# A gate/up product in seven block products (Strassen) instead of eight, with the trunk in DRAM during a feed-forward part

## The chip, the cores and the metric

The kernel runs on one core of one Trainium2 chip. The metric is device time in microseconds. Matrix products run on TensorE, elementwise work on VectorE and ScalarE, a little on GpSimd, and every DMA is issued by SyncE, in order, on one queue.

## The reference

Two layers of a diffusion trunk over 640 tokens: 512 of the sample and 128 of the prompt, width 1024, all in float32. Each layer has a feed-forward part (FFN), a token mix (two kinds of attention and a Fourier branch) and a second FFN; each of the three is followed by a LayerNorm over the sum with the trunk. Nine vectors per layer (the adaLN vectors: shift, scale and gate) come from a product of the conditioning vector with `w_mod`. An FFN with 2816 hidden columns is

```python
g, u = jnp.split(h @ w_gu, 2, axis=-1)
return (jax.nn.silu(g) * u) @ w_down
```

so that four FFNs run in all, and they hold most of the arithmetic.

## The kernel before

Activations lie transposed: 8 row blocks of 128 channels by 640 tokens, and the tokens in two halves of 320. A float32 product is made of rounded parts: `Unit` loads a weight block of up to 128 x 1024 and splits it into `hi`, cast by ScalarE (L149), and `lo`, the rest, subtracted by VectorE (L154); activations are split in the same way (`vsplit`, L109 and L110; `hh` and `hl` are the two parts of the input, `midh` and `midl` those of the hidden columns). `mm3` (L112) then issues three matmuls for each block of 128 x 128 weights and 320 tokens: hi by hi (L113), hi by the activations' lo (L114) and lo by hi (L115).

`ffn_steps` (L586) cuts the 2816 hidden columns into 22 tiles of 128. A tile's body multiplies 8 row blocks by the gate weights and 8 by the up weights, for two halves: 8 x 2 x 2 x 3 = 96 matmuls. `finish` (L593) applies SiLU on ScalarE and the product with `u` on VectorE (L599), and splits the result. After the first 11 tiles their part of the down product is formed, column by column (8 columns `m`, 11 x 2 x 3 matmuls each), and `plain_residual` (L711) adds it into the trunk, which stays in SBUF. After the other 11 tiles comes the second down part, with the LayerNorm: the last two columns are formed for half 0, then for half 1, so that half 0's LayerNorm can run beside half 1's matmuls (`LayerNorm.skewed`, L454); the last LayerNorm of all ends in the output (`finale`).

The conditioning work is spread through this. A `mod` of `mod_steps` (L254) is one 512 KB slice of `w_mod`, which VectorE multiplies and adds in two instructions of 1024 (L268 for the first slice of a vector, L270 for the others); after eight slices TensorE adds up and transposes (L274, L286), and VectorE writes the vector (L291). `with_mods` (L1723) places the slices evenly over the steps of an FFN.

The program is written as a list of steps, each with the weight units that it needs. `prep_to` (L162) loads and splits units ahead, at most `LOOK` = 4 units beyond the step, in rings of three raw and four hi/lo buffers. A scheduler then orders the instructions of each engine; the engines run theirs in order and wait on semaphores. Before a first FFN `startup` puts `w_mod` blocks into six slots; the token mix uses the rings' and the trunk's space for its own tiles.

Of the kernel before, what the change touches and what calls it, by code (L numbers as in the profile page):

```python
# [20 lines left out]
KT = 8  # L21
DEPTH = 2
NS = 512
# [5 lines left out]
PARTS = (11, 11)  # L29
MIDW = 11 * T  # L30
T_BUFS = 7
# [4 lines left out]
LOOK = 4  # L36
# [5 lines left out]
RAW_BUFS = 3  # L42
# [14 lines left out]
def trunk_kernel(ctx: ExitStack, tc: tile.TileContext, a, y_prompt, y_sample, new_a_k, new_a_v, new_b_k, new_b_v):  # L57
# [58 lines left out]

    class Unit:
# [3 lines left out]

        def prep(self):
            self.load()
            self.convert()

        def load(self):
            w = self.k * self.n
            if self.extra:
                raw = big.tile([128, 3 * T], F32, tag="xr", name="xr")[:, :w]
            else:  # L130
                raw = ring.tile([128, 1024], F32, tag="raw", name="raw")[:, :w]
# [9 lines left out]
        def high(self):  # L141
# [4 lines left out]
            else:  # L146
                hi = ring.tile([128, 1024], F32R, tag="hi", name="hi", bufs=HI_BUFS)[:, :w]
# [5 lines left out]
        def low(self):  # L153
            nc.vector.tensor_sub(self.l, self.raw, self.h)  # L154

# [6 lines left out]
    def prep_to(n):  # L162
        while ptr[0] < min(n, len(flat)):
            flat[ptr[0]].prep()
            ptr[0] += 1

# [3 lines left out]
    def step(units, fn):  # L170
        steps.append((units, fn, False))
# [23 lines left out]
    rope = const.tile([128, 2, NS], F32, name="rope")  # L195
# [58 lines left out]
    def mod_steps(l, j):  # L254
        out = []
        for k in range(KT):
# [3 lines left out]
            def fn(u=u, k=k):  # L260
# [10 lines left out]
                if k == KT - 1:  # L271
# [21 lines left out]
            out.append(([u], fn, False))  # L293
# [292 lines left out]
    def ffn_steps(l, which, gate_fn, pre=None):  # L586
        wgu = a[f"w_ffn{which}_gu"][l]
        wdn = a[f"w_ffn{which}_down"][l]
        gu = lambda t: (wunit(wgu, 0, KT, t * 128, 128), wunit(wgu, 0, KT, FFN + t * 128, 128))
        loc = {}  # L590
        ln = LayerNorm(l, 0 if which == 1 else 2, gate_fn)

        def finish(i, pg, pu):  # L593
            mh, ml = loc["mid"]
# [3 lines left out]
            for src, v in pu.pieces():  # L598
                nc.vector.tensor_mul(v(s), v(s), src)  # L599
            vsplit(mh[:, i, :], ml[:, i, :], s)  # L600
            return s
# [5 lines left out]

        t = 0
        for pi, n in enumerate(PARTS):
            for i in range(n):  # L610
                if t == 0:
# [16 lines left out]
                    steps.append(([u0[0], u0[1], u1[0]], head, bool(pre)))  # L628

                    def second(u1=u1):  # L630
# [3 lines left out]
                        finish(1, loc.pop("g1"), pu)  # L634

                    step([u1[1]], second)
                elif t > 1:
                    u = gu(t)

                    def body(u=u, i=i, last=(t == FT - 1)):  # L640
# [7 lines left out]
                        s = finish(i, pg, pu)  # L648
                        if last:
                            preload_rsqrt(s[:, 0:1])  # L650
                        if state["rescale"]:
                            state["rescale"].pop(0)()

                    step(list(u), body)
                t += 1
            k0 = t - n
            ka = n // 2
            final = pi == len(PARTS) - 1
            du = lambda m: [wunit(wdn, k0, ka, m * 128, 128), wunit(wdn, k0 + ka, n - ka, m * 128, 128)]

            def down_mm(us, out, hf, n, ka):
                mh, ml = loc["mid"]
                for k in range(n):
                    u, kk = (us[0], k) if k < ka else (us[1], k - ka)
                    mm3(out, u.h[:, kk, :], u.l[:, kk, :], mh[:, k, half(hf)], ml[:, k, half(hf)], k == 0, k == n - 1)

            nskew = (3 if ln.last else 2) if final else 0
            for m in range(KT - nskew):
                us = du(m)

                def body(us=us, m=m, n=n, ka=ka, final=final):
# [5 lines left out]
                    for hf in range(2):  # L677
                        down_mm(us, p.h[hf], hf, n, ka)
                    for hf in range(2):
                        if final:  # L680
                            ln.residual(m, hf, p.h[hf])
                        else:
                            plain_residual(m, hf, p.h[hf], gate_fn())

                step(us, body)
            if final:
                us = [wunit(wdn, k0 + k, min(4, n - k), (KT - 2) * 128, 256) for k in range(0, n, 4)]
                at = {(m, k): (us[k // 4], k % 4, 128 * (m - KT + 2)) for m in (KT - 2, KT - 1) for k in range(n)}
                if ln.last:
                    us = du(KT - 3) + us  # L690
                    us[0].extra = True
# [1136 lines left out]
```

## Time and profile before

| | us |
|---|---|
| three runs | 2567.93, 2566.44, 2567.11 (median 2567.11) |
| profiled execution, first to last instruction (its span) | 2563.8 |
| median less that span | 3.3 |
| TensorE busy | 2529.4 (99%) |
| VectorE busy | 1476.9 (58%) |
| ScalarE busy | 931.5 (36%) |
| mean granted clock of TensorE | 0.997 |

The profiled execution gives no time of its own beside its span; the span and the 3.3 us around it make up the median. Matmul records overlap, so the busy time of TensorE says when it has work and not how fast that work goes.

### The profile page before, as it was taken

Reading aid. Unit: us, or ns where it says so; the run is one execution under the profiler, and the core shown is the slowest. Engines: PE = TensorE matmul, PEld = TensorE weight load, DVE = VectorE, ACT = ScalarE, POOL = GpSimd, SP = SyncE. Lnnn points to the kernel's source line nnn. Section 1 sums busy time; section 2 is a strip of 40 time slices with the busy share of each in tenths; the row PEclk is TensorE's granted clock in tenths of the full one; section 3 lists DMA queues with packets and bytes.
Section 4 is the critical chain, followed back from the end, with each engine's and each line's share of the span. In section 5 each row is a group of like instructions: output and inputs, shape, how many; then the busy total and the mean of one; then the engine's idle time right before and its main releaser. Section 6 shows DMA issues by size and latency. Waiting matters only on the chain.

```text
span 2563.8 us, 41715 instructions
## 1 busy us (share of the span) xinstructions
PE 2529.4 (99%) x17407; PEld 2453.6 (96%) x17407; DVE 1476.9 (58%) x2522; ACT 931.5 (36%) x1714; POOL 40.3 (2%) x42
## 2 busy tenths in 40 slices
PE   8999999999999999999999999999999999999998
PEld 6999999999979999999999999999998899999998
DVE  5555644767967634433684465568678684232335
ACT  4221222366775421222262212225567662212221
POOL 0000000001100000000000000000110000000000
PEclk9999999999999999999999999999999999999999
DMA  9444543333122423433333354433411324122221
GB/s 265 144 122 134 156 124 106 116 121 86 35 84 88 141 74 101 123 91 94 111 107 116 106 157 136 132 114 107 125 50 49 113 75 132 56 85 83 71 83 56
DMA packets 371033, 273.64 MB, mean 107 GB/s; under 512 B 11162, under 2 KB 347804, under 8 KB 370332
## 3 DMA queue, kind: packets, MB, share of 16 engines
q1 hardware_dynamic: 370844, 270.98, 36.4%
q8 instruction: 136, 2.23, 0.4%
q14 instruction: 53, 0.43, 0.1%
HBM read 254.95 MB, written 9.18 MB: 103 GB/s over the span
## 4 chain that ended last, share of the span: by engine, by line
PE 89%; DVE 5%; ACT 2%; DMA 2%; SPq 1%; issue 1%; DVEq 0%; ACTq 0%
PE g L113 8%; PE g L114 8%; PE u L115 8%; PE g L115 8%; PE u L113 8%; PE u L114 8%; PE d L113 7%; PE d L114 7%; PE d L115 7%; PE b_o L1315 1%; PE a_o L1174 1%; PE o L113 1%; PE o L114 1%; PE o L115 1%; PE ps_v L937 1%; PE ps_v L938 1%
## 5 line engine op out<-in xcount | busy, mean ns | idle before, releaser
L149 ACT CAST hi<-raw 128x1024 fp32r<-128x1024 f32 (+4 forms) x355 | 336.6, 951 | 1249.2 <-PE u L114 414.6
L154 DVE TENSOR_TENSOR lo<-raw,hi 128x1024 fp32r<-128x1024 f32 (+4 forms) x355 | 390.0, 1100 | 371.1 <-ACT hi L149 369.8
L115 PE MATMUL u<-hh,lo 128*128 128x320 f32 x1408 | 435.2, 309 | 0.4 <-DVE lo L154 0.4
L114 PE MATMUL u<-hl,hi 128*128 128x320 f32 x1408 | 435.5, 309 | 0.0
L113 PE MATMUL u<-hh,hi 128*128 128x320 f32 x1408 | 435.2, 309 | 0.0
L113 PE MATMUL g<-hh,hi 128*128 128x320 f32 x1344 | 417.0, 310 | 0.0
L113 PE MATMUL d<-midh,hi 128*128 128x320 f32 x1342 | 416.1, 310 | 0.0
L115 PE MATMUL g<-hh,lo 128*128 128x320 f32 x1344 | 415.8, 309 | 0.0
L114 PE MATMUL g<-hl,hi 128*128 128x320 f32 x1344 | 415.2, 309 | 0.0
L114 PE MATMUL d<-midl,hi 128*128 128x320 f32 x1342 | 415.0, 309 | 0.0
L115 PE MATMUL d<-midh,lo 128*128 128x320 f32 x1342 | 414.8, 309 | 0.0
L270 DVE SCALAR_TENSOR_TENSOR acc<-raw,csil,acc 128x1024 f32<-128x1024 f32 x224 | 279.0, 1281 | 159.8 <-DMA raw<-in_w_mod_dram 159.7
L115 PEld LDWEIGHTS u<-hh,lo 128*128 128x128 f32 x1408 | 264.3, 188 | 0.8 <-DVE lo L154 0.6
L114 PEld LDWEIGHTS u<-hl,hi 128*128 128x128 f32 x1408 | 264.3, 188 | 0.2
L113 PEld LDWEIGHTS u<-hh,hi 128*128 128x128 f32 x1408 | 264.3, 188 | 0.0
L113 PEld LDWEIGHTS g<-hh,hi 128*128 128x128 f32 x1344 | 252.3, 188 | 8.0 <-issue 7.1
L113 PEld LDWEIGHTS d<-midh,hi 128*128 128x128 f32 x1342 | 251.9, 188 | 6.1 <-ACT hi L149 3.4
L115 PEld LDWEIGHTS g<-hh,lo 128*128 128x128 f32 x1344 | 252.3, 188 | 0.2
L114 PEld LDWEIGHTS g<-hl,hi 128*128 128x128 f32 x1344 | 252.3, 188 | 0.0
L114 PEld LDWEIGHTS d<-midl,hi 128*128 128x128 f32 x1342 | 251.9, 188 | 0.2
L115 PEld LDWEIGHTS d<-midh,lo 128*128 128x128 f32 x1342 | 251.9, 188 | 0.0
L599 DVE TENSOR_TENSOR silu<-silu,u 128x320 f32<-128x320 f32 x176 | 84.9, 486 | 255.6 <-PE u L115 254.1
(530 smaller groups left out, 3705.8 us busy)
## 6 DMA issues: line engine op xcount, KB each, us to landing
raw<-in_w_ffn_gu_dram SPq DMA_DIRECT2D x172, 512.0 KB
raw<-in_w_mod_dram SPq DMA_DIRECT2D x128, 512.0 KB
raw<-in_w_ffn_down_dram SPq DMA_DIRECT2D x60, 384.0 KB
raw<-in_w_ffn_down_dram SPq DMA_DIRECT2D x55, 320.0 KB
raw<-in_w_in_dram SPq DMA_DIRECT2D x24, 512.0 KB
raw<-in_w_out_dram SPq DMA_DIRECT2D x16, 512.0 KB
vtile<-vtile SPq DMA_DIRECT2D x40, 160.0 KB
st_midh<-in_w_mod_dram SPq DMA_DIRECT2D x10, 512.0 KB
```

Source lines behind the costliest of these rows:

```text
L113: nc.tensor.matmul(out, wh, xh, start=first, stop=False)
L114: nc.tensor.matmul(out, wh, xl, start=False, stop=False)
L115: nc.tensor.matmul(out, wl, xh, start=False, stop=last)
L149: nc.scalar.copy(hi, self.raw.rearrange("p k n -> p (k n)"))
L154: nc.vector.tensor_sub(self.l, self.raw, self.h)
L270: nc.vector.scalar_tensor_tensor(acc[:, s, :], w, cs, acc[:, s, :], op0=ALU.mult, op1=ALU.add)
L599: nc.vector.tensor_mul(v(s), v(s), src)
L937: nc.tensor.matmul(ps, hh[:, k, c], wh, start=(k == 0), stop=False)
L938: nc.tensor.matmul(ps, hl[:, k, c], wh, start=False, stop=False)
L1174: nc.tensor.matmul(x["po"][64 * r : 64 * r + 64, :128], M["va"][:, kt, 64 * g : 64 * g + 64], ph[:, c0 : c0 + 128], start=(kt == 0), stop= ...
L1315: nc.tensor.matmul(x["po"][:, 128 * q : 128 * q + 128], ph[:, c0 : c0 + 128], M["vb"][:, kt, 128 * h : 128 * h + 128], start=(kt == 0 and ...
```

## The change

Of an FFN's 22 tiles the first 10 (first FFN) or 5 (second FFN) stay as they were; the other 12 or 17 go through `seven`, 58 tiles in all. There the 8 row blocks are two groups of four (inputs' rows 1 and 2), and the two halves of tokens, and gate and up columns, make 2 x 2 blocks. Strassen's scheme (in Winograd's form) forms the four results from seven products of block sums, each of 4 row blocks x 3 matmuls = 12. `Pair` loads a gate and an up block into two raw buffers, splits the gate block and the second half of the up block, and then overwrites the raw buffers with sums of the blocks (`Sums`, split in their turn). `block_sums` makes the matching sums of activations: `t12` lies in the trunk's buffer, `t4` in a buffer called `xr`, and `t3` replaces the second half of the first four row blocks of `hh` and `hl` (`block_third`). Some products add into the PSUM tile of an earlier one, once VectorE or ScalarE has read the earlier value.

Since the trunk's buffer is taken, the trunk lies in DRAM during an FFN: eight tiles of 320 KB are stored (`park`), one is fetched, added to and stored again for each column of a down part that is not the last, and all return ahead of the last (`unpark`). The down product has three parts, of 8, 7 and 7 tiles. The `w_mod` slices are placed by rates: three to a plain tile, 1.25 and 1.75 to a column of the first FFN's down parts, one in the second FFN's, none in the tiles of seven products. Weights are prepared ahead as far as counts of held raw and hi/lo buffers allow (`advance`), with four raw buffers in place of three. The rope table is fetched into a ring buffer in each token mix instead of once, startup uses five slots, and some tiles of attention lie elsewhere.

```diff
-PARTS = (11, 11)
-MIDW = 11 * T
-T_BUFS = 7
+PARTS = (8, 7, 7)
+MIDW = max(PARTS) * T
+PLAIN = {1: 10, 2: 5}
+MOD_RATE = {1: (3.0, 1.25, 1.75), 2: (3.0, 1.0, 1.0)}
+T_BUFS = 9
...
-RAW_BUFS = 3
+RAW_BUFS = 4
...
+    class Pair(Unit):
+        def __init__(self, gate_src, up_src):
+            super().__init__(None, KT, 128)
+            self.pair = gate_src, up_src
+            self.raws = 2
+
+        def fetch(self):
+            self.g, self.u = (ring.tile([128, 1024], F32, tag="raw", name="raw") for _ in range(2))
+            for t, src in ((self.g, self.pair[0]), (self.u, self.pair[1])):
+                nc.sync.dma_start(out=t.rearrange("p (k n) -> p k n", k=KT), in_=src)
+
+        def convert(self):
+            held["raw"] += 1
+            self.raw = self.g.rearrange("p (k n) -> p k n", k=KT)
+            self.high()
+            u2 = ring.tile([128, 512], F32R, tag="hi2", name="hi2", bufs=2)
+            l2 = ring.tile([128, 512], F32R, tag="lo2", name="lo2", bufs=2)
+            g1, g2, u1, up = self.g[:, :512], self.g[:, 512:], self.u[:, :512], self.u[:, 512:]
+            nc.scalar.copy(u2, up)
+            self.low()
+            nc.vector.tensor_sub(l2, up, u2)
+            self.h2, self.l2 = (x.rearrange("p (k n) -> p k n", k=4) for x in (u2, l2))
+            nc.vector.tensor_add(up, up, u1)
+            nc.vector.tensor_add(u1, u1, g1)
+            nc.vector.tensor_add(g1, g1, up)
+            nc.vector.tensor_add(g2, g2, g1)
...
+        def convert(self):
+            self.raw = getattr(self.pair, self.which).rearrange("p (k n) -> p k n", k=KT)
+            self.high()
+            self.low()
...
+    def room(u):
+        return u.early and (u.loaded or held["raw"] + u.raws <= RAW_BUFS)
+
+    def advance():
+        while ptr[0] < len(flat):
+            u = flat[ptr[0]]
+            if not room(u) or u.extra or held["hi"] + u.his > HI_BUFS:
+                break
+            prep_to(ptr[0] + 1)
+        for u in flat[ptr[0] :]:
+            if not room(u):
+                break
+            u.load()
...
+        def park(n):
+            for _ in range(n):
+                state["rescale"].pop(0)()
+                k = KT - 1 - len(state["rescale"])
+                nc.sync.dma_start(out=parked[k], in_=state["trunk"][:, k, :])
+
+        def fetch(m):
+            xt[m] = t640(f"xt{m}")
+            nc.sync.dma_start(out=xt[m], in_=parked[m])
+
+        def unpark():
+            new_trunk()
+            for k in range(KT):
+                nc.sync.dma_start(out=state["trunk"][:, k, :], in_=parked[k])
...
+        def block_sums(k):
+            if k == 0:
+                t12 = big.tile([128, KT * T], F32R, tag="trunk", name="t12")
+                t4 = big.tile([128, 4 * T], F32R, tag="xr", name="t4")
+                loc["t12"] = [x.rearrange("p (k t) -> p k t", k=4) for x in (t12[:, : 4 * T], t12[:, 4 * T :])]
+                loc["t4"] = [x.rearrange("p (k t) -> p k t", k=4) for x in (t4[:, : 4 * HW], t4[:, 4 * HW :])]
+                loc["t3"] = []
+            if k % 2 == 0:
+                loc["t3"].append(t640(f"t3_{k}"))
+            t3 = loc["t3"][k // 2][:, half(k % 2)]
+            hh, hl = state["hh"], state["hl"]
+            f, g = t640(f"tf{k}"), t640(f"tg{k}")
+            nc.vector.tensor_add(f, hh[:, k, :], hl[:, k, :])
+            nc.vector.tensor_add(g, hh[:, k + 4, :], hl[:, k + 4, :])
+            f0, f1, g0, g1 = f[:, :HW], f[:, HW:], g[:, :HW], g[:, HW:]
+            nc.vector.tensor_sub(t3, g1, f1)
+            nc.vector.tensor_sub(f0, f0, f1)
+            nc.vector.tensor_add(f1, f0, g1)
+            nc.vector.tensor_sub(g0, f1, g0)
+            vsplit(loc["t12"][0][:, k, :], loc["t12"][1][:, k, :], f)
+            vsplit(loc["t4"][0][:, k, :], loc["t4"][1][:, k, :], g0)
+
+        def block_third():
+            for i, t3 in enumerate(loc["t3"]):
+                dh, dl = (state[key][:, 2 * i : 2 * i + 2, HW:] for key in ("hh", "hl"))
+                vsplit(dh, dl, two(t3))
+
+        def seven(i, us, last):
+            pair, sg, su = us
...
+            ab = mmp.tile([128, 2, 512], F32, tag="mm", name="ab")
+            cd = mmp.tile([128, 2, 512], F32, tag="mm", name="cd")
+            pa, pb, pc, pd = ab[:, 0, :HW], ab[:, 1, :HW], cd[:, 0, :HW], cd[:, 1, :HW]
+            u, s = t640("up"), t640("silu")
+            product(pa, g, 0, h, 0, c0)
+            nc.scalar.copy(u[:, c1], pa)
+            product(pb, gg, 0, t12, 0, c1)
+            nc.vector.tensor_sub(u[:, c0], pb, u[:, c1])
+            product(pc, uu, 4, t12, 0, c0)
+            nc.vector.tensor_sub(u[:, c1], u[:, c0], pc)
+            product(pd, uu, 0, h, 0, c1)
+            nc.vector.tensor_sub(u[:, c1], u[:, c1], pd)
+            su.release()
+            advance()
+            product(pa, g, 4, h, 4, c0, False)
+            nc.scalar.activation(s[:, c0], pa, AF.Silu)
+            pair.release()
+            advance()
+            product(pc, gg, 4, h, 4, c1, False)
+            nc.vector.tensor_sub(s[:, c1], pc, u[:, c0])
+            nc.scalar.activation(s[:, c1], s[:, c1], AF.Silu)
+            product(pd, u2, 0, t4, 0, c0, False)
+            nc.vector.tensor_sub(u[:, c0], u[:, c0], pd)
+            nc.vector.tensor_mul(s, s, u)
+            keep(i, s)
...
+                        if which == 2 and t >= plain - 2:
+                            for k in range(2):
+                                block_sums(2 * (t - plain + 2) + k)
+                        if t == plain - 1:
+                            block_third()
...
+                    if not final:
+                        nc.sync.dma_start(out=parked[m], in_=xt.pop(m))
+                        if m + 2 < KT:
+                            fetch(m + 2)
+                    if which == 1 and pi == 0 and m % 2 == 1:
+                        block_sums(m // 2)
...
+        due = 0.0
+        for s in main:
             steps.append(s)
-            want = min(len(ms), max(int(math.ceil(per * (i + 1 - first))), min(KT, i + 1 - first)))
-            while done < want:
-                steps.append(ms[done])
-                done += 1
-        steps.extend(ms[done:])
+            due += s[3]
+            while ms and due >= 1.0:
+                steps.append(ms.pop(0))
+                due -= 1.0
```

The order of the instructions is shown at three places. First, VectorE in the second FFN of layer 0, before: a plain tile has a split of the gate and one of the up weights (L154), two products with `u` (L599) and the split of the hidden tile (L110).

```order
L154 TENSOR_TENSOR lo<-raw,hi 128x1024
L110 TENSOR_TENSOR midl<-silu,midh 128x640
L154 TENSOR_TENSOR lo<-raw,hi 128x1024
L599 TENSOR_TENSOR silu<-silu,u_9173 128x320
L599 TENSOR_TENSOR silu<-silu,u_9174 128x320
L154 TENSOR_TENSOR lo<-raw,hi 128x1024
L110 TENSOR_TENSOR midl<-silu,midh 128x640
```

In the changed kernel the same engine in a tile of seven products, in the same FFN; `up` and `silu` are the tile's intermediate results, `ab` and `cd` its two PSUM tiles, L195 to L198 the sums of weights. A split of the hidden tile (L111) and the first sum of the next tile's weights follow.

```order
L749 TENSOR_TENSOR up<-ab,up 128x320
L198 TENSOR_TENSOR raw<-raw 128x512
L751 TENSOR_TENSOR up<-up,cd 128x320
L753 TENSOR_TENSOR up<-up,cd 128x320
L165 TENSOR_TENSOR lo<-raw,hi 128x1024 x2
L761 TENSOR_TENSOR silu<-cd,up 128x320
L165 TENSOR_TENSOR lo<-raw,hi 128x1024
L764 TENSOR_TENSOR up<-up,cd 128x320
L193 TENSOR_TENSOR lo_10429<-raw,hi_10428 128x512
L765 TENSOR_TENSOR silu<-silu,up 128x640
L195 TENSOR_TENSOR raw<-raw 128x512
L196 TENSOR_TENSOR raw<-raw 128x512
```

A tile's work has gone from five instructions to fifteen, and results of TensorE are read at five points of it in place of two.

Second, VectorE in the same FFN where its first adaLN vector is done, before: the vector is written (L291) between the work of plain tiles.

```order
L154 TENSOR_TENSOR lo<-raw,hi 128x1024
L110 TENSOR_TENSOR midl<-silu,midh 128x640
L291 TENSOR_TENSOR mods_113<-ps_modt_8_9299,vec_105 128x8 x2
L729 TENSOR_SCALAR gate_9732<-mods_113 128x16
L154 TENSOR_TENSOR lo<-raw,hi 128x1024
L599 TENSOR_TENSOR silu<-silu,u_9313 128x320
L599 TENSOR_TENSOR silu<-silu,u_9314 128x320
L154 TENSOR_TENSOR lo<-raw,hi 128x1024
```

The changed kernel at the same point, which is now the entry into its first tile of seven products; `tf` and `tg` are activation sums in work, `t_9043` is `t12`, `t_9044` is `t4`, `t_0_9045` and `t_2_9185` are the `t3` that go over `hh` and `hl`. The rows end with the splits of weight sums.

```order
L719 TENSOR_TENSOR tf_9198<-tf_9198 128x320
L111 TENSOR_TENSOR hl<-t_0_9045,hh 128x2x320
L111 TENSOR_TENSOR midl<-silu,midh 128x640
L720 TENSOR_TENSOR tf_9198<-tf_9198,tg_9199 128x320
L111 TENSOR_TENSOR hl<-t_2_9185,hh 128x2x320
L721 TENSOR_TENSOR tg_9199<-tf_9198,tg_9199 128x320
L111 TENSOR_TENSOR t_9043<-tf_9198,t_9043 128x640
L111 TENSOR_TENSOR t_9044<-tg_9199,t_9044 128x320
L198 TENSOR_TENSOR raw<-raw 128x512
L362 TENSOR_TENSOR mods_112<-ps_modt_8_9265,vec_104 128x8 x2
L339 TENSOR_SCALAR acc_0_9272<-raw,csil 128x1024 x2
L165 TENSOR_TENSOR lo<-raw,hi 128x1024 x3
```

The activation sums, the weight sum L198, the vector and two first slices now stand ahead of the splits (L165) that the first tile needs.

Third, SyncE in the first FFN of layer 0, before, in a down part: weights and slices of `w_mod` alternate.

```order
L134 DMA raw<-in_w_ffn_down_dram 128x5x128
L134 DMA raw<-in_w_ffn_down_dram 128x6x128
L134 DMA raw<-in_w_mod_dram 128x1024
L134 DMA raw<-in_w_ffn_down_dram 128x5x128
L134 DMA raw<-in_w_ffn_down_dram 128x6x128
L134 DMA raw<-in_w_mod_dram 128x1024 x2
L134 DMA raw<-in_w_ffn_down_dram 128x5x128
L134 DMA raw<-in_w_ffn_down_dram 128x6x128
```

The changed kernel in its second down part; `xt` is a trunk tile on its way between DRAM and a residual.

```order
L144 DMA raw<-in_w_ffn_down_dram 128x7x128
L144 DMA raw<-in_w_mod_dram 128x1024 x2
L678 DMA xt_3227<-park_131 128x640
L144 DMA raw<-in_w_ffn_down_dram 128x7x128
L144 DMA raw<-in_w_mod_dram 128x1024
L678 DMA xt_3297<-park_132 128x640
L144 DMA raw<-in_w_ffn_down_dram 128x7x128
L870 DMA park_127<-xt_3059 128x640
L144 DMA raw<-in_w_mod_dram 128x1024
L870 DMA park_128<-xt_3061 128x640
```

The fetches (L678) and stores (L870) of trunk tiles stand among the loads, and each column has one down weight where it had two.

## Rows read from the trace of the kernel before

**Rows 1.** Page, part 1: engine, busy us (share of the span), instructions.
```profile
PE 2529.4 (99%) x17407; PEld 2453.6 (96%) x17407; DVE 1476.9 (58%) x2522; ACT 931.5 (36%) x1714; POOL 40.3 (2%) x42
```

**Rows 2.** Page, part 4: shares of the chain that ended last, by engine.
```profile
PE 89%; DVE 5%; ACT 2%; DMA 2%; SPq 1%; issue 1%; DVEq 0%; ACTq 0%
```

**Rows 3.** TensorE's waits: waited for, us in all, times, longest us.
```profile
PE ps_m L795 <- DMA st_midh<-in_w_mod_dram: 2.9, 3, 2.0
...
PE u L115 <- DVE lo L154: 0.4, 1, 0.4
```

**Rows 4.** Timeline of TensorE, 351 us: start us, us, engine, line, operation.
```profile
351.25 0.31 PE L114 MATMUL g<-hl,hi 128*128 128x320 f32 x1
351.39 0.31 PE L115 MATMUL g<-hh,lo 128*128 128x320 f32 x1
351.54 0.31 PE L113 MATMUL g<-hh,hi 128*128 128x320 f32 x1
351.69 0.31 PE L114 MATMUL g<-hl,hi 128*128 128x320 f32 x1
```

**Rows 5.** Stretches: us, busy (x instructions) by engine, PEclk granted clock, DMA share.
```profile
10.00:20.00 10.00, 6.97 (x51) 4.95 (x50) 4.57 (x9) 2.62 (x4) 0.00 (x0) 0.74 1.21 290
80.00:90.00 10.00, 7.83 (x54) 7.51 (x53) 6.57 (x16) 1.66 (x3) 0.00 (x0) 1.00 0.61 177
140.00:200.00 60.00, 60.00 (x412) 59.99 (x412) 35.20 (x41) 13.35 (x18) 0.00 (x0) 1.00 0.44 125
516.00:526.00 10.00, 9.23 (x57) 8.10 (x56) 10.00 (x25) 8.33 (x18) 0.00 (x0) 1.00 0.28 86
```

**Rows 6.** VectorE by line and shape: count, busy us, mean ns, idle before.
```profile
L270 DVE SCALAR_TENSOR_TENSOR acc<-raw,csil,acc 128x1024 f32<-128x1024 f32 x224 | 279.0, 1281 | 159.8 <-DMA raw<-in_w_mod_dram 159.7
...
L154 DVE TENSOR_TENSOR lo<-raw,hi 128x1024 fp32r<-128x1024 f32 x222 | 271.6, 1225 | 238.7 <-ACT hi L149 238.1
...
L599 DVE TENSOR_TENSOR silu<-silu,u 128x320 f32<-128x320 f32 x176 | 84.9, 486 | 255.6 <-PE u L115 254.1 <-ACT silu L597 1.4
...
L110 DVE TENSOR_TENSOR midl<-silu,midh 128x640 fp32r<-128x640 f32 x88 | 72.0, 819 | 0.0
...
L268 DVE TENSOR_SCALAR acc<-raw,csil 128x1024 f32<-128x1024 f32 x32 | 23.0, 748 | 11.7 <-PE g L115 6.1 <-DMA raw<-in_w_mod_dram 4.9 <-PE ps_mod L274 0.7
...
L714 DVE SCALAR_TENSOR_TENSOR trunk<-d,gate,trunk 128x320 f32<-128x320 f32 x32 | 17.6, 550 | 49.7 <-PE d L115 49.7
...
L714 DVE SCALAR_TENSOR_TENSOR trunk<-d,gate,trunk 128x192 f32<-128x192 f32 x32 | 13.2, 412 | 10.6 <-PE d L115 10.6
...
L714 DVE SCALAR_TENSOR_TENSOR trunk<-d,gate,trunk 128x128 f32<-128x128 f32 x32 | 10.9, 342 | 0.0
...
L1029 DVE TENSOR_TENSOR qb_r<-qb_r,qb_s 128x512 f32<-128x512 f32 x8 | 5.5, 684 | 0.2
```

**Rows 7.** ScalarE by line and shape, columns as in the group before.
```profile
L149 ACT CAST hi<-raw 128x1024 fp32r<-128x1024 f32 x222 | 232.6, 1050 | 796.9 <-PE u L114 336.1 <-PE g L114 308.8 <-PE d L114 87.4
...
L109 ACT CAST midh<-silu 128x640 fp32r<-128x640 f32 x88 | 63.6, 722 | 17.4 <-DVE silu L599 17.0
```

**Rows 8.** DMA: page, the queue over the span; 20 to 40 us, rate by slice.
```profile
q1 hardware_dynamic: 370844, 270.98, 36.4%
...
GB/s 291 289 293 287 292 289 291 289 293 289 293 287 292 289 293 311 345 359 373 377 389 390 360 326 308 296 292 290 290 292 292 290 283 267 271 285 296 265 286 287
```

**Rows 9.** End of layer 0's first FFN: TensorE, then VectorE, columns as in group 4.
```profile
522.56 0.41 PE L113 MATMUL hk<-hh,xh 128*128 128x320 f32 x1 [0.74 <-ACT hh L109]
...
516.12 1.22 DVE L154 TENSOR_TENSOR lo<-raw,hi 128x1024 fp32r<-128x1024 f32 x1
...
523.08 0.48 DVE L423 SCALAR_TENSOR_TENSOR ln_y<-ln00m,ln_y 128x320 f32<-128x320 f32 x1
...
523.48 0.48 DVE L429 TENSOR_TENSOR trunk<-trunk,ln00ds 128x320 f32<-128x320 f32 x1
```

More of the change, by code (lines that the diff above doesn't have):

```diff
@@ L35 @@
 RMS_EPS = 1e-6
-LOOK = 4
 KF = 258
@@ L115, in mm3, with mm3s @@
         nc.tensor.matmul(out, wl, xh, start=False, stop=last)
+    def mm3s(out, wh, wl, xh, xl, first, last):
+        nc.tensor.matmul(out, wh, xh, start=first, stop=False, skip_group_check=True)
+        nc.tensor.matmul(out, wh, xl, start=False, stop=False, skip_group_check=True)
+        nc.tensor.matmul(out, wl, xh, start=False, stop=last, skip_group_check=True)
+    held = {"raw": 0, "hi": 0}
     class Unit:
@@ L120, in __init__ @@
             self.extra = False
-        def prep(self):
-            self.load()
-            self.convert()
+            self.loaded = self.released = False
+            self.raws, self.his = 1, 1 if split else 0
+            self.early = True
         def load(self):
[L127 to L131, printed above, removed]
+            if self.loaded:
+                return
+            self.loaded = True
+            held["raw"] += self.raws
+            self.fetch()
+        def fetch(self):
+            raw = ring.tile([128, 1024], F32, tag="raw", name="raw")[:, : self.k * self.n]
             self.raw = raw.rearrange("p (k n) -> p k n", k=self.k)
@@ L591, in ffn_steps @@
         ln = LayerNorm(l, 0 if which == 1 else 2, gate_fn)
+        plain = PLAIN[which]
+        rates = MOD_RATE[which]
+        parked = [dram.tile([128, T], F32, tag=f"park{l}{which}{k}", name=f"park{l}{which}{k}") for k in range(KT)]
+        xt = {}
+        def park(n):
[10 more added lines that the diff above has]
+                nc.sync.dma_start(out=state["trunk"][:, k, :], in_=parked[k])
         def finish(i, pg, pu):
-            mh, ml = loc["mid"]
             s = t640("silu")
@@ new lines, in block_third, with product @@
+        def block_third():
[4 more added lines that the diff above has]
+            pair, sg, su = us
+            hh, hl = state["hh"], state["hl"]
+            t12, t4 = loc["t12"], loc["t4"]
+            c0, c1 = slice(0, HW), slice(HW, T)
+            def product(out, w, kw, x, kx, c, first=True):
+                for k in range(4):
+                    mm3s(out, w[0][:, kw + k, :], w[1][:, kw + k, :], x[0][:, kx + k, c], x[1][:, kx + k, c], first and k == 0, k == 3)
+            g, gg, uu, u2 = (pair.h, pair.l), (sg.h, sg.l), (su.h, su.l), (pair.h2, pair.l2)
+            h = hh, hl
+            ab = mmp.tile([128, 2, 512], F32, tag="mm", name="ab")
[22 more added lines that the diff above has]
+            nc.vector.tensor_mul(s, s, u)
+            keep(i, s)
+            if last:
+                preload_rsqrt(s[:, 0:1])
@@ new lines, in body @@
+                        if t == plain - 1:
+                            block_third()
+                    step(list(u), body, rates[0])
+                elif t >= plain:
+                    pair = Pair(cols(t * 128), cols(FFN + t * 128))
+                    us = [pair, Sums(pair, "g"), Sums(pair, "u")]
+                    def body(us=us, i=i, t=t):
+                        if i == 0:
+                            new_mid()
+                        seven(i, us, t == FT - 1)
+                        if t == FT - 1:
+                            unpark()
+                    step(us, body)
@@ L655, in ffn_steps, with more @@
+                if i == n - 1 and not final:
+                    last_gu = steps[-1]
+                    def more(fn=last_gu[1]):
+                        fn()
+                        fetch(0)
+                        fetch(1)
+                    steps[-1] = (last_gu[0], more, *last_gu[2:])
                 t += 1
             k0 = t - n
-            ka = n // 2
-            final = pi == len(PARTS) - 1
-            du = lambda m: [wunit(wdn, k0, ka, m * 128, 128), wunit(wdn, k0 + ka, n - ka, m * 128, 128)]
```

150 lines of the change are left out of this document (85 added, 65 removed).

## The prediction

> **What bounds the kernel now.** I read the page's busy times first, then the chain of waits, then TensorE's waits and the rate of its matmuls, last the durations on the engines beside it. TensorE is busy for 99% of the span, VectorE for 58%, ScalarE for 36% [rows 1], and 89% of the chain that ends last is TensorE [rows 2]. Its longest sum of waits is 2.9 us, at startup; in the gate/up products it waits 0.4 us for a low part in the whole run [rows 3]. So time falls only by TensorE's own work, and every new wait shows in full.
>
> What one matmul costs is not in its duration column. Each is listed with 0.31 us, yet the next starts after 0.14 to 0.15 us [rows 4]: they overlap. Over a long stretch, 412 in 60.00 us make 145.6 ns [rows 5]. That stretch holds some narrower ones; the starts themselves, three in 0.44 us, make 146.6 ns, which I use. The 0.31 us would overstate the gain twofold.
>
> **The matmuls that go.** A plain gate/up tile has 8 row blocks x 2 halves x (gate, up) x 3 = 96 matmuls, a tile of seven products 7 x 4 x 3 = 84. There are 12 new tiles in each first and 17 in each second FFN, 58 in all: 58 x 12 = 696 matmuls x 0.1466 = **102.0 us**. The down product keeps 22 x 8 x 2 x 3 per FFN.
>
> By the Trainium skill, "TensorE: Matmul & The Clock Gate", Back-to-back issue gap, an isolated matmul takes columns/2.4 ns plus 2.5, which for 320 columns is an estimate of 135.8 ns and would make this term 94.5 us. The page adds that weight loads share the pace in a real stream; the trace has 146.6, and that decides.
>
> **A tile of seven products in steady state.** TensorE needs 84 x 0.1466 = 12.31 us. VectorE gets three splits of 1024, five operations of 512, five of 320 and two of 640 (first pair of order pieces): 3 x 1.225 + 5 x 0.684 + 5 x 0.486 + 2 x 0.819 = 11.16 us [rows 6]. In a row they cost 0.08 less each (starts 0.40 apart, duration 0.48 [rows 9]): 10.0 us, 81%. ScalarE has three casts of 1.05, one of half that, a copy and two SiLU of 320 (under 0.5 each) and one cast of 0.72: some 6.2 us [rows 7]. Loads are 1.05 MB in 12.3 us, 85 GB/s, where the queue moves 270.98 MB in 36.4% of 2563.8 us, 290 GB/s while it is busy [rows 8]. All stay below TensorE, and the releases come three to four us ahead of need, so I put the steady state at TensorE's pace: 0. Upper bound: VectorE in full series with what it waits for, 1 us per tile or more; that is a rival below.
>
> **Entries into the new tiles.** The first new tile needs sums of activations and weights that nothing has prepared ahead. In the second FFN of layer 0 the second pair of order pieces shows what VectorE still does after the last plain matmul: four operations of 640 (0.74 each, less the 0.08), five of 320 (0.40; one, a product with u, just ahead of the piece), the last weight sum (0.60), two first adaLN slices (0.748 - 0.08) and the first low part (1.15): 2.96 + 2.0 + 0.6 + 1.34 + 1.15 = 8.05 us, and some 2.8 us of ScalarE casts inside that chain (two of 0.72, one of 1.05 and releases), 10.9. TensorE can cover it with the first product (12 x 0.1466 = 1.76) and about 1.1 us of adaLN matmuls. So it waits about 8 us there, in front of the third matmul of the second product; behind it stand all later products, since TensorE takes them in order. In layer 1 the sums come earlier in the queue: about 4. In the first FFNs the activation sums are made during the down part, and only two casts and splits of 640, one weight sum, one cast and one low part follow the last plain matmul, about 5.3 us against 1.8 of cover: 3.5 each. Sum 8 + 4 + 2 x 3.5 = **19 us**. At the later returns to new tiles (after the down parts) the weights have mostly been converted, except in the first FFNs at tile 15, where a cast waits behind adaLN work: 2.5 x 2 = **5**. The trace has no such hand-over; the nearest hole is the 2.17 us of idle at 81 to 84 us, within a slice in which TensorE has 7.83 of 10 [rows 5]. Below: 0, if the scheduler's order runs earlier than I read it. Above: 11 at each of the four entries and 4 at each of eight returns, 76.
>
> **LayerNorm tails.** Half 0's LayerNorm hides behind half 1's matmuls of the last two down columns. Eleven row blocks gave 66, seven give 42: cover 9.7 falls to 6.2 us, 3.5 less. VectorE is full there already (10.00 of 10) [rows 5], and TensorE waits 0.74 us at the boundary [rows 9]. One split of 1.22 us inside it [rows 9] goes, so about 2.3 us each at three ends, and 1.5 at the finale, which is VectorE's and the stores' own time: **8.4**. From 0 to 14.
>
> **Down parts, parking and w_mod.** A column of the first part is 48 matmuls, 7.04 us; VectorE has one split 1.225, three residual pieces 0.550 + 0.412 + 0.342, 1.25 adaLN slices of 2 x 1.281, and in the first FFNs half of a block sum (three operations of 640 and five of 320 make 4.9, four sums in eight columns): 1.225 + 1.304 + 3.20 + 2.45 = 8.2, less 0.08 for each of 10.5 instructions, 7.3 [rows 6]. In the second part 42 matmuls, 6.16 us; VectorE 1.1 (the split of 896 by its width) + 1.3 + 3.5 x 1.281 - 0.6 = 6.3. So it lags by 0.1 to 0.3 us a column, 3 us per first FFN, partly taken up by lead: 2.5 x 2, and 1.5 x 2 in the second FFNs, whose rate is lower: **8**. Parking adds 640 KB a column. With w_mod a column of the second part asks for 448 + 1.75 x 512 + 640 KB = 2.03 MB in 6.16 us, 330 GB/s. The queue gave 290 with weight columns and 311 to 390 where wide rows were under way [rows 8]; three quarters here are wide rows, so I price it at 0, up to 0.8 us a column at 290 (13 in both first FFNs). SyncE issues in order: a store of a parked tile waits for its residual, and behind it stand w_mod slices, the next fetch and the next down weights (third pair). Two tiles are fetched ahead, so a lag of one column is hidden.
>
> By the Trainium skill, "DMA: Bandwidth & Descriptors", Where 436 GB/s comes from, HBM gives one core about 358 GB/s; the 330 would then just fit, and the trace's 390 in one slice is above that figure. Term: 0 by page and by row alike, 13 by the 290 alone.
>
> **Clock.** Between 10 and 20 us, with TensorE busy 6.97 of 10, the granted clock was 0.74; around the 2.2 us hole it was 1.00 [rows 5]. Holes of 4 to 8 us may fall in between: 26% of a 10 us slice is 2.6 us, at perhaps one entry: **2**, bounds 0 and 10. Startup with one slot fewer, attention with its buffers moved, and rope fetched per layer: VectorE, ScalarE and TensorE work is the same, the loads lie 0 to 4 us off either way; 0.
>
> **Sum.** 19 + 5 + 8.4 + 8 + 2 = 42.4 us come back of 102.0; net 59.6. The profiled execution has a span of 2563.8 us; the median of the three runs is 2567.1, so 3.3 lie around the span and stay. Forecast 2563.8 - 59.6 + 3.3 = **2507.5 us**.
>
> **Rivals.**
> *Nearly all is hidden.* The order of instructions is the scheduler's, and ScalarE and VectorE idle 64% and 42% now [rows 1]. If only the tails and 4 us more are lost, 2567.1 - 102.0 + 12.4 = 2477.5. For: the existing waits are tiny [rows 3]. Against: the queue of VectorE at the entries, read row by row.
> *Parking and the queue in the down parts bind.* Two parked parts x 8 columns x 4 FFNs = 64 columns; at 0.6 us a column beyond my sum (0.8 is the bound at 290 GB/s) 38 us more: 2546. For: VectorE at or above TensorE's time in the first FFNs. Against: the second FFNs have 0.25 to 0.75 slices less a column, and two tiles of lead.
> *Slower: hand-overs inside the new tile.* Four products add into a bank that VectorE or ScalarE must first have read, and TensorE takes its products in order. If VectorE is in a 1.2 us split when the bank is ready, TensorE can wait for 1.2 + 0.4 us. It has 12 to 36 other matmuls in between (1.8 to 5.3 us), against a VectorE loaded at 81%. With 42.4 us back elsewhere the change loses from 59.6 / 58 = 1.03 us a tile; one exposed split in each tile gives 58 x 1.2 = 70 us more: 2577. Half of that, 2542, stays faster.
> *It doesn't do what it says:* excluded, since the changed program lists 16,136 matmuls where the old one lists 16,832, 696 fewer.
>
> **Chances.** My sum (2490 to 2528) 0.60; nearly all hidden 0.18; parking binds, or half-exposed splits (2528 to 2562) 0.14; within 0.2% (5.1 us, about what a measurement of this kernel can tell from no change) 0.03; slower 0.05. Faster is 0.60 + 0.18 + 0.14 = 0.92. The range 2472 to 2540 leaves out the worse part of parking, no change and slower, and the case without any loss (2465).
>
> **What would show it.** Matmuls should start 0.1466 us apart in the new tiles, with 12.3 us from tile to tile; more means that the hand-overs cost. TensorE's largest waits should name low parts of weight sums or activation sums at four places, 3 to 8 us each, and ln or hh at three. VectorE's share should rise from 58% to some 75%. If waits of TensorE total under 20 us, I over-read the queues; if many small ones name VectorE's split in all tiles, or a DMA of down weights, the second or third rival was right.

## The result: slower by 2.2%, where 2.3% faster was forecast

| | before | changed |
|---|---|---|
| median, us | 2567.5 | 2621.8 |
| ratio (95% interval) | | 1.022 (1.0206 to 1.0235) |
| span of the profiled execution | 2563.8 | 2620.2 |
| forecast, range | | 2507.5, 2472 to 2540 |

The matmuls went as planned: TensorE has 17407 - 16711 = 696 fewer [rows 1], 102.0 us at the rate of [rows 4]. So 56.4 us more of span mean that 158.4 us were given back, where the prediction had 42.4.

The first line is part 1 of the page of the changed kernel, the second part 4, the shares of the chain that ended last. They answer to [rows 1, 2]. The shares of the chain add up to 43%, because the profile follows it back only as far as 1480 us, so they can't be set against [rows 2] one by one.

```profile
PE 2492.8 (95%) x16711; PEld 2363.5 (90%) x16711; DVE 1941.6 (74%) x3306; ACT 1079.2 (41%) x1958; POOL 43.9 (2%) x42
...
PE 28%; DVE 9%; ACT 3%; DMA 2%; issue 1%; SPq 0%; DVEq 0%; ACTq 0%
```

TensorE is still busy for 95%, although it does 4% less in a longer span. An overlapped matmul of 0.31 us counts whole when a pause follows it, so this share hides short pauses. What it waits for shows better; these are the largest waits of TensorE (waited for, us in all, times, longest), where [rows 3] had 2.9 us at the top.

```profile
PE ab L119 <- DVE up L749: 34.2, 38, 5.2
PE cd L119 <- DVE up L764: 16.3, 31, 0.5
PE ps_modt L357 <- ACT mod_sb L354: 9.1, 5, 2.8
PE ps_mod L345 <- DVE acc L341: 7.1, 8, 2.0
...
PE ab L119 <- ACT hi L160: 3.5, 1, 3.5
```

Two reads by VectorE inside the tile of seven products lead (`pa` and `pb` are the halves of the PSUM tile `ab`, `pc` and `pd` those of `cd`). But for one of 5.2 us they are short, and their count is high: the loss lies in most of the 58 tiles and not at a few entries. In a stretch of such tiles, the product with `u` (L765) starts at 413.91, 428.18, 442.44 and 456.71 us: 14.27 us a tile, where its matmuls make 12.31 and a plain tile 14.07. A tile with 12 matmuls fewer takes 0.2 us longer than a plain one.

The pauses of such a tile in the timeline of TensorE (start, duration, idle before in brackets):

```profile
435.00 0.31 PE L121 MATMUL cd<-hh,lo 128*128 128x320 f32 x1
...
435.59 0.31 PE L121 MATMUL ab<-hh,lo 128*128 128x320 f32 x1
435.89 0.41 PE L119 MATMUL cd<-hh,hi 128*128 128x320 f32 x1
436.15 0.31 PE L120 MATMUL cd<-hl,hi 128*128 128x320 f32 x1
...
440.98 0.31 PE L121 MATMUL cd<-t,lo 128*128 128x320 f32 x1
441.13 0.31 PE L121 MATMUL ab<-hh,lo 128*128 128x320 f32 x1
441.97 0.39 PE L119 MATMUL cd<-t,hi 128*128 128x320 f32 x1 [0.53 <-DVE up L764]
442.19 0.31 PE L120 MATMUL cd<-t,hi 128*128 128x320 f32 x1
...
445.41 0.31 PE L121 MATMUL cd<-t,lo 128*128 128x320 f32 x1
446.38 0.42 PE L119 MATMUL ab<-hh,hi 128*128 128x320 f32 x1 [0.66 <-DVE up L749]
446.64 0.31 PE L120 MATMUL ab<-hl,hi 128*128 128x320 f32 x1
```

And VectorE beside it:

```profile
435.35 0.49 DVE L753 TENSOR_TENSOR up<-up,cd 128x320 f32<-128x320 f32 x1 [2.29 <-PE cd L121]
...
441.33 0.49 DVE L764 TENSOR_TENSOR up<-up,cd 128x320 f32<-128x320 f32 x1 [1.01 <-PE cd L121]
...
443.90 0.69 DVE L196 TENSOR_TENSOR raw<-raw 128x512 f32<-128x512 f32 x1
444.51 0.82 DVE L111 TENSOR_TENSOR midl<-silu,midh 128x640 fp32r<-128x640 f32 x1
445.24 0.68 DVE L197 TENSOR_TENSOR raw<-raw 128x512 f32<-128x512 f32 x1
445.85 0.48 DVE L749 TENSOR_TENSOR up<-ab,up 128x320 f32<-128x320 f32 x1
```

First pause, at 441.13: the last matmul of a tile's product into pd (half of the PSUM tile `cd`) starts at 440.98; one matmul follows; the next tile's first product into its own `cd` has to wait until VectorE has read the old pd (L764, begun at once). From start to start 0.84 us in place of 0.147. Second pause, at 445.41: the product that adds to pa waits until VectorE has read **pb** (L749), which it doesn't need, but which lies in the same PSUM tile `ab`. VectorE does three other operations first. 0.97 us in place of 0.147. A third pause, at 435.59 (the first rows), is small: the product that adds to pc waits for VectorE's read of **pd** (L753, done at 435.84), again the other half of its tile; 0.30 us in place of 0.147. With restarts (0.22 to 0.26 us to the second matmul after each pause) the three make the 1.95 us over 12.31.

VectorE's own operations are as expected from [rows 6]; by line and shape (count, busy us, mean ns, idle before):

```profile
L165 DVE TENSOR_TENSOR lo<-raw,hi 128x1024 fp32r<-128x1024 f32 x308 | 375.0, 1222 | 91.2 <-ACT hi L160 88.6
L341 DVE SCALAR_TENSOR_TENSOR acc<-raw,csil,acc 128x1024 f32<-128x1024 f32 x224 | 278.8, 1279 | 13.5 <-DMA raw<-in_w_mod_dram 13.4
```

### The profile page after: what moved, and what is told of

Its sections match the earlier page's. It is cut to its first block, busy times and chain, and to the rows that moved or that the text cites. A ratio compares the mean times of both kernels' runs of the same rounds, so it can differ in the third digit from the quotient of the medians.

```text
span 2620.2 us, 41901 instructions
## 1 busy us (share of the span) xinstructions
PE 2492.8 (95%) x16711; PEld 2363.5 (90%) x16711; DVE 1941.6 (74%) x3306; ACT 1079.2 (41%) x1958; POOL 43.9 (2%) x42
## 3 DMA queue, kind: packets, MB, share of 16 engines
q1 hardware_dynamic: 400364, 334.43, 42.4%
## 5 line engine op out<-in xcount | busy, mean ns | idle before, releaser
L165 DVE TENSOR_TENSOR lo<-raw,hi 128x1024 fp32r<-128x1024 f32 (+4 forms) x386 | 455.4, 1185 | 114.8 <-ACT hi L160 111.3
L341 DVE SCALAR_TENSOR_TENSOR acc<-raw,csil,acc 128x1024 f32<-128x1024 f32 x224 | 278.8, 1279 | 13.5 <-DMA raw<-in_w_mod_dram 13.4
L119 PE MATMUL ab<-hh,hi 128*128 128x320 f32 x464 | 148.8, 321 | 34.8 <-DVE up L749 34.2
L119 PE MATMUL cd<-t,hi 128*128 128x320 f32 x464 | 149.0, 321 | 19.8 <-DVE up L764 16.3
L119 PE MATMUL cd<-hh,hi 128*128 128x320 f32 x464 | 150.7, 325 | 1.4 <-DVE up L751 0.6
L116 PE MATMUL u<-hh,lo 128*128 128x320 f32 x480 | 148.5, 309 | 0.5 <-DVE lo L165 0.5
L115 PE MATMUL u<-hl,hi 128*128 128x320 f32 x480 | 148.6, 310 | 0.0
L114 PE MATMUL u<-hh,hi 128*128 128x320 f32 x480 | 148.5, 309 | 0.0
L121 PE MATMUL ab<-hh,lo 128*128 128x320 f32 x464 | 144.4, 311 | 0.8 <-DVE lo L165 0.7
L120 PE MATMUL ab<-hl,hi 128*128 128x320 f32 x464 | 145.0, 313 | 0.0
L121 PE MATMUL cd<-hh,lo 128*128 128x320 f32 x464 | 144.2, 311 | 0.0
L120 PE MATMUL cd<-hl,hi 128*128 128x320 f32 x464 | 144.1, 311 | 0.0
L120 PE MATMUL cd<-t,hi 128*128 128x320 f32 x464 | 143.9, 310 | 0.0
```

What stands on the lines that cost most here:

```text
L114: nc.tensor.matmul(out, wh, xh, start=first, stop=False)
L115: nc.tensor.matmul(out, wh, xl, start=False, stop=False)
L116: nc.tensor.matmul(out, wl, xh, start=False, stop=last)
L119: nc.tensor.matmul(out, wh, xh, start=first, stop=False, skip_group_check=True)
L120: nc.tensor.matmul(out, wh, xl, start=False, stop=False, skip_group_check=True)
L121: nc.tensor.matmul(out, wl, xh, start=False, stop=last, skip_group_check=True)
```

## Experiments

Two theories stood against each other: **H**, that PSUM tiles shared by two accumulators make TensorE wait for reads, and **V**, that VectorE's fifteen operations in order set the period. **P**, the rival of the prediction, had parking and the down parts.

### A PSUM tile for each accumulator: e1, e2, e3

```diff
-            ab = mmp.tile([128, 2, 512], F32, tag="mm", name="ab")
-            cd = mmp.tile([128, 2, 512], F32, tag="mm", name="cd")
-            pa, pb, pc, pd = ab[:, 0, :HW], ab[:, 1, :HW], cd[:, 0, :HW], cd[:, 1, :HW]
+            pa, pb = (mmp.tile([128, 2, 512], F32, tag="mm", name=x)[:, 0, :HW] for x in ("pa", "pb"))
+            pc, pd = (proj_bank(x)[:, :HW] for x in ("pc", "pd"))
```

That is e1; `proj_bank` gives single banks that the tiles of seven products didn't use. e2 keeps `ab` and takes `pc, pd` from `proj_bank`; e3 takes `pa, pb` from `proj_bank` and keeps `cd`, with an unused tile allocated ahead of it, so that `cd` stays in the same buffer.

> The four accumulators of a tile of seven products get a PSUM tile each instead of two tiles of two. Theory H (hand-overs of PSUM tiles): in the changed kernel a steady tile takes 14.26 us, of which 12.31 are matmuls; 0.82 us go to a wait of the product that adds to pa for the read of pb (L749, same PSUM tile), 0.69 to a wait of the next pc for the read of the last pd (L764, same tile), the rest to restarts. With a tile each both waits go: 12.3 to 12.8 us a tile, 58 x 1.5 to 1.95 = 87 to 113 us less, about 2510 to 2535. Theory V (VectorE's 15 operations in order set the period, whatever the banks): the period stays above 13.5 us and the time above 2575.

> Only pc and pd get a PSUM tile each; pa and pb still share one. Theory H: the wait for L764 goes, the wait for L749 stays; 0.7 to 0.9 us a tile, some 40 to 52 us less: 2570 to 2582. Theory V: no change, about 2620.

> Only pa and pb get a PSUM tile each; pc and pd still share one, and an unused tile keeps it in the same buffer from tile to tile. Theory H: the wait for L749 goes, that for L764 may stay; 0.8 to 1.3 us a tile, some 46 to 75 us less: 2546 to 2576. Theory V: no change, about 2620.

| | median, us | ratio to before (95% interval) | steady tile, us |
|---|---|---|---|
| changed | 2621.8 | 1.022 (1.0206 to 1.0235) | 14.27 |
| e1, four tiles | 2527.9 | 0.9847 (0.9833 to 0.9862) | 12.32 |
| e2, pc and pd apart | 2538.6 | 0.989 (0.9875 to 0.9904) | 12.51 |
| e3, pa and pb apart | 2543.5 | 0.991 (0.9895 to 0.9925) | 12.2 to 12.8 |

H holds and V falls: with the same fifteen operations on VectorE the tile takes TensorE's 12.31 us. One edit of PSUM tiles is worth 2621.8 - 2527.9 = 93.9 us. But the two waits don't add, as I had expected of e2 (2570 to 2582) and e3 (2546 to 2576): each edit alone brings 78 to 83 us. The timeline of e2 shows why. Its TensorE, then its VectorE:

```profile
433.95 0.31 PE L119 MATMUL pd<-hh,hi 128*128 128x320 f32 x1
434.39 0.31 PE L119 MATMUL ab<-hh,hi 128*128 128x320 f32 x1
...
432.07 0.48 DVE L749 TENSOR_TENSOR up<-ab,up 128x320 f32<-128x320 f32 x1
```

`ab` is still shared here, and L749 still comes late. But the scheduler, which now sees no wait at `cd`, has put the product into pd ahead of the one that adds to pa, so L749 is done 1.8 us before it is needed. In the changed kernel the product into pa came straight after pc. What one wait costs thus depends on how many matmuls the order leaves in front of it. The order alone, with the shared tiles kept, wasn't tried.

### VectorE's queue ahead of the read: v1

The changed kernel without these four lines:

```diff
-            nc.vector.tensor_add(up, up, u1)
-            nc.vector.tensor_add(u1, u1, g1)
-            nc.vector.tensor_add(g1, g1, up)
-            nc.vector.tensor_add(g2, g2, g1)
```

> The changed kernel with its shared PSUM tiles, but the four sums of weight blocks (L195 to L198) are left out, so the products use unsummed blocks; VectorE has 2.4 us less in each tile and nothing of it stands ahead of the read of pb except the split of the hidden tile. Theory Q (the wait at L749 is VectorE's queue ahead of the read, the wait at L764 is the bare hand-over without cover): the tile falls from 14.26 to about 13.2 to 13.5, the wait for L764 stays at 0.5 to 0.7 in each tile. Theory B (a shared tile costs both hand-overs in full, whatever VectorE does): the tile stays at 14.2.

One run, 2555.3 us; the steady tile takes 12.79 us, less than theory Q's 13.2 to 13.5. Its wait for pb's read (L745 there):

```profile
PE ab L119 <- DVE up L745: 4.8, 5, 1.9
```

38 waits have become 5, although the order has eight matmuls in front of that add where the changed kernel had ten. So the wait was VectorE's queue ahead of the read, as theory Q says. The wait at pd's read shrank too, against Q: a pause of 0.15 us is left, since the order now has four matmuls in front of that product in place of one. So the longer wait, for pb's read, needed three things together: a shared tile (gone in e1 and e3), a read that stands late in VectorE's queue (gone in v1), and an order with too few matmuls between (gone in e2). For pd's read the second wasn't needed: VectorE began it at once.

### The rest without new tiles: p1

```diff
-PLAIN = {1: 10, 2: 5}
+PLAIN = {1: FT, 2: FT}
```

and no `block_sums` or `block_third`; `unpark` and `preload_rsqrt` go to the last plain tile.

> All 88 tiles are plain, and the activation sums are left out; the trunk in DRAM, the down product in three parts, the rates of the w_mod slices (three to every plain tile, so they are done earlier) and the moved buffers stay. Theory H: what comes back outside the tiles of seven products is the LayerNorm tails and the down parts, 8 + 8 us of the prediction: about 2575 to 2592. Theory P (parking and the parts cost most of the 156 us that were lost): 2620 or more.

2586.4 us, ratio 1.0075 (1.0058 to 1.0092): 20.2 us over before, and P falls. By stretches, half of it is in the token mixes: 310.8 and 309.8 us, where before had 305.1 and 304.3. The prediction had put their changed buffers at 0. The other half isn't split here between parking, the three down parts and the slices.

### Slices of w_mod, and the entries: g1, n1, g2

g1 is e1 with `MOD_RATE = {1: (4.0, 1.25, 1.0), ...}`. n1 is e1 with `PLAIN = {1: 10, 2: 6}` and the second FFNs' sums in tiles 3 and 4:

```diff
-                        if which == 2 and t >= plain - 2:
+                        if which == 2 and plain - 3 <= t < plain - 1:
                             for k in range(2):
-                                block_sums(2 * (t - plain + 2) + k)
+                                block_sums(2 * (t - plain + 3) + k)
```

> e1_four_banks with the first FFN's w_mod rates at 4, 1.25 and 1 slices (in place of 3, 1.25 and 1.75), so that fewer slices lie in the second down part. In e1 the way from the end of tile 14 to that of tile 15 in the first FFNs takes 73.8 and 73.1 us, where 42 x 8 + 84 matmuls and 1.75 adaLN vectors need about 64; the second FFNs need 63. Theory L (late slices hold the raw buffers and VectorE, so that tile 15's weights come late): 8 us less there, twice; up to 2 us more in the plain tiles; together 10 to 16 us less than e1, 2512 to 2518. Theory O (the hole at tile 15 comes from the down part's own traffic, parking included): under 4 us.

> e1_four_banks with the second FFNs' activation sums one tile earlier (in tiles 3 and 4), and one tile more plain there (6 in place of 5). The extra plain tile costs 1.76 us each, 3.5 in all. In e1 the first eight tiles of a second FFN take 121.1 and 121.3 us where their matmuls need about 109 to 110. Theory E (the entry waits for activation sums that queue on VectorE): 5 to 8 us less at each entry, net 6 to 12 us less than e1. Theory W (the entry waits for the weights' sums and splits, whatever the activations do): no gain at the entry, net 2 to 4 us more than e1.

> Both edits of g1_rates and n1_sums_early on e1_four_banks. If both theories L and E hold, the gains add: 16 to 28 us less than e1, 2500 to 2512; if only L holds, 2514 to 2520; if only E, 2516 to 2522.

| | median, us | ratio to before (95% interval) |
|---|---|---|
| e1 | 2527.9 | 0.9847 (0.9833 to 0.9862) |
| g1 | 2519.6 | 0.9813 (0.9798 to 0.9827) |
| n1 | 2523.6 | 0.9827 (0.9811 to 0.9843) |
| g2, both | 2516.8 | 0.9804 (0.9789 to 0.982) |

Theory L names the place: tile 14 to tile 15 in the first FFNs falls from 73.8 and 73.1 us to 64.2 and 62.7. Half of that comes back elsewhere: 5.7 us from tile 8 to tile 14 (87.3 and 84.4 us for 82.8 and 83.2), 3.0 from tile 0 to tile 7 and 2.0 behind tile 15. So the sum is 8 us and not 10 to 16. n1 is 4 us under e1 by its median, less than the 6 to 12 of theory E and not W's loss, but their intervals overlap. g2 lies where L alone or E alone was to put it, and its interval overlaps g1's: that n1's edit brings anything in all is not shown. In the traces the entry of layer 1 fell from 121.3 to 117.9 us although it has a plain tile more; that of layer 0 stayed (121.1 and 121.5), and what holds it is open.

How such a hole looks, in e1 at tile 15's entry: TensorE's timeline, then its windows (length, PE, PEld, VectorE, ScalarE, GpSimd busy, granted clock, DMA share, GB/s).

```profile
369.52 0.30 PE L119 MATMUL pa<-hh,hi 128*128 128x320 f32 x1
373.52 1.92 PE L345 MATMUL ps_mod<-acc,ones 128*32 128x512 f32 x4 [3.69 <-DVE acc L341]
375.37 0.64 PE L120 MATMUL pa<-hl,hi 128*128 128x320 f32 x1
...
364.00:368.00 4.00, 4.00 (x28) 3.77 (x26) 2.79 (x6) 1.05 (x1) 0.00 (x0) 1.00 0.94 268
368.00:372.00 4.00, 1.12 (x6) 0.74 (x5) 2.26 (x4) 0.62 (x1) 0.00 (x0) 0.99 0.50 143
372.00:376.00 4.00, 2.48 (x6) 0.82 (x7) 4.00 (x8) 0.04 (x1) 0.00 (x0) 0.50 0.00 0
376.00:380.00 4.00, 4.00 (x16) 2.00 (x15) 4.00 (x4) 3.63 (x5) 0.00 (x0) 0.65 0.62 197
```

A sum of adaLN slices stands in TensorE's queue in the middle of a product whose weights are there, and everything behind it waits 3.7 us for VectorE's work on the last slice. Meanwhile the granted clock falls: it is 0.50, the lower level (1.2 GHz), from 372 to 376 us and 0.65 on the mean from 376 to 380, where TensorE is busy throughout and gets through 16 matmuls, four of them a wider adaLN sum. Before the hole 28 fit into 4 us.

### Moving work away: g3, g4

g3 is g2 with the six sums of `block_sums` as `nc.gpsimd` operations. g4 is g2 with `rope` as a constant tile loaded once, and `T_BUFS = 7`.

> g2_both with the six additions and subtractions of each activation block sum on GpSimd (the splits stay on VectorE and ScalarE). In g2 the first down part of the first FFNs takes 79.8 us from tile 7 to tile 8, where its matmuls and its adaLN vector need about 72.5; VectorE is busy 95% there. Theory D (VectorE's load in that part costs these 7 us): 3.3 us of VectorE's work go for each of four sums, 4 to 7 us less in each first FFN, 8 to 14 less in all: 2503 to 2509. Theory G (GpSimd's own time, 1.5 us for 512 columns in the trace of before, makes the sums later than VectorE would, above all in the second FFNs' entry): 0 to 15 us more than g2.

> g2_both with the rope table loaded once into its own buffer again, so that in the token mix one more hi buffer of the ring is free; seven temporary tiles in place of nine make the room. The two mixes take 309.8 us each in g2 and 305.1 and 304.3 in before. Theory R (the ring with fewer buffers and the table's load make the mixes longer): 4 to 5 us less in each, 8 to 10 in all, 2507 to 2509, if seven temporary tiles are enough elsewhere. Theory S (the other moved tiles or the order of the scheduler make them longer): within 3 us of g2.

g3: 2534.3 us, ratio 0.988 (0.9865 to 0.9895), 17.5 us slower than g2: theory G, a little beyond its 15. The first down part didn't get shorter (80.7 and 82.0 us for 79.8 and 79.9), so D falls; the eight tiles from 0 to 7 of layer 1's second FFN take 101.0 us for 91.4. Its GpSimd and VectorE by line (count, busy us, mean ns, idle before):

```profile
L715 POOL TENSOR_TENSOR tf<-hh,hl 128x640 f32<-128x640 f32 x16 | 38.2, 2388 | 927.2 <-DVE midl L111 474.1 <-DVE trunk L502 278.1 <-PE ps_modt L357 132.2
L718 POOL TENSOR_TENSOR t<-tg,tf 128x320 f32<-128x320 f32 x16 | 21.1, 1320 | 49.6 <-issue 24.4 <-DMA park<-xt 17.9 <-DVE t L111 7.3
...
L341 DVE SCALAR_TENSOR_TENSOR acc<-raw,csil,acc 128x1024 f32<-128x1024 f32 x224 | 308.4, 1413 | 12.6 <-DMA raw<-in_w_mod_dram 12.4
```

g4: 2513.5 us, ratio 0.98 (0.9782 to 0.9817). The mixes fall from 309.8 to 307.9 and 307.8 us, 3.9 in all: less than theory R wanted, a little more than S allows; its interval overlaps g2's. It is the best version of this study by its median: 52 us under before in the same runs, where the change as given is 54 over. What the rest of the mixes' 10 us is stays open.

## Why the prediction was wrong

**The step that failed** is the steady state: "All stay below TensorE, and the releases come three to four us ahead of need, so I put the steady state at TensorE's pace: 0." It is 14.27 us a tile in place of 12.31, and with e1 it costs 93.9 us in all. I had weighed the releases of weight buffers and not those of PSUM. The right mechanism stood among the rivals, hand-overs inside the tile, at 58 x 1.2 = 70 us and a chance of 5%. I rejected it because TensorE "has 12 to 36 other matmuls in between". That held for each accumulator by itself. By PSUM tile it was wrong: pa shares with pb, which VectorE reads ten matmuls before, with three operations queued ahead; pc shares with pd, whose first value ends four matmuls before the add to pc and whose last ends one matmul before the next pc. These waits could be read off the program's order beforehand, as the instructions in front of each add on TensorE and in front of each read on VectorE.

This step alone takes the forecast out of its range: e1, without these waits, takes 2527.9 us, within 2472 to 2540. That is still 20 us over the forecast: of the 102.0 us e1 gives back 63.7 (2527.9 against 2566.2 for before in its runs), where 42.4 were forecast. The rival's 2577 was 45 us too low for the same two reasons: 93.9 for its 70, and those 21 us.

The other terms, against stretches from tile to tile (from the start of VectorE's split of one hidden tile to that of another), e1 against p1 with 1.76 us taken off p1 for each tile of seven:

| step | predicted | measured |
|---|---|---|
| matmuls removed | -102.0 | 696 fewer, at 146.6 ns in steady tiles (e1: 12.32 us for 84) |
| steady tiles | 0 | +93.9 (changed less e1) |
| entries, second FFNs | 12 | 15.6 (121.1 + 121.3 for 118.5 + 118.9, three tiles each) |
| entries, first FFNs | 7 | 9.3 (82.8 + 83.2 for 87.2 + 87.1, five tiles each) |
| tile 15, first FFNs | 5 | 20.0 (73.8 + 73.1 for 2 x 65.2, slices of w_mod included) |
| first down part, first FFNs | 5 | 8.0 (78.9 + 77.8 for 74.3 + 74.4) |
| down parts, second FFNs | 3 | none seen (69.3 + 69.8 for 74.0 + 70.4, a tile of seven in each) |
| LayerNorm tails and finale | 8.4 | none seen |
| mixes | 0 | 10.4 (309.9 twice for 305.1 and 304.3) |

These rows are the terms of the prediction and not a full account: what p1 loses in the FFNs against before isn't among them. The entries were about right. Tile 15 was low: in e1 the sum of the last slice held it for 3.7 us in layer 0, a low part of weights for 0.7, and the lower clock followed; g1, with fewer slices there, takes 20 us off that place. The tails were wrong: from tile 21's split to the first matmul of the token mix before takes 80.7 us, of which 528 matmuls make 77.4 and two adaLN sums the rest; the changed kernel takes 48.8 us for 336 matmuls, 49.3. The 3.5 us of cover less cost nothing. VectorE is as full as I had it in the last 10 us ahead of the boundary at 540.00 (9.91 busy) but not from 524 to 534 us (7.48); that its work found room there is an argument, and no run tests it. The changed kernel's windows (columns as above):

```profile
524.00:534.00 10.00, 9.60 (x61) 8.66 (x59) 7.48 (x19) 4.35 (x10) 0.00 (x0) 1.00 0.21 76
...
530.00:540.00 10.00, 8.82 (x55) 7.74 (x53) 9.91 (x26) 6.97 (x16) 0.00 (x0) 1.00 0.26 85
```

The wait at the boundary is the old one, 0.74 us in [rows 9]; in the changed kernel's timeline:

```profile
540.00 0.41 PE L114 MATMUL hk<-hh,xh 128*128 128x320 f32 x1 [0.73 <-ACT hh L110]
```

Parking shows in no wait of TensorE, as predicted: none names a fetched or stored trunk tile in the changed kernel's list. The clock, priced at 2, did fall at holes; the changed kernel's windows at the second FFN's entry (columns as above) have 0.88 and 0.55. What that cost isn't separated here from the holes themselves.

```profile
918.00:924.00 6.00, 1.89 (x13) 1.36 (x11) 6.00 (x13) 2.89 (x6) 0.00 (x0) 0.88 0.00 0
924.00:930.00 6.00, 4.78 (x18) 4.30 (x19) 5.33 (x10) 3.25 (x4) 0.00 (x0) 0.55 0.54 145
```

Two of the signs to look for came: more than 12.3 us from tile to tile ("more means that the hand-overs cost"), and VectorE's share at 74%, where "some 75%" was expected. The one for the third rival ("if many small ones name VectorE's split in all tiles") came nearly so: many small waits, which name VectorE's reads.

## What to carry to other kernels

A product with fewer matmuls is worth its count only if every add into an accumulator finds its PSUM tile already read: for each one, count the matmuls in front of it on TensorE and the operations in front of the read on the reading engine. Give each accumulator its own PSUM tile when banks are free, since here each wait was for the whole tile. Judge a dense stretch by the time from tile to tile and not by the busy share, which stayed at 95% while a seventh of each new tile was lost.

## What the runs showed of the hardware

GpSimd took 2.39 us on the mean for a sum of 128 x 640 (g3); VectorE does an operation of that size in 0.82 [rows 6]. While GpSimd worked, VectorE was slower: its slices of w_mod rose from 1.280 us in g2 to 1.413 in g3 on the mean over all 224. That mean hides the effect: the 177 that meet no sum on GpSimd take 1.28 us, as in g2, the 20 that lie wholly within such sums 2.28 on the mean.

After each of the pauses shown inside a tile the second matmul starts 0.22 to 0.26 us after the first, in place of 0.147. Half the granted clock came with a wait of 3.7 us in the middle of dense work (e1); at that level matmuls of 320 columns start 0.27 us apart, from 375.81 to 376.61 us.
